# Feed-forward of an encoder layer on one core: one pass over three blocks of 768 tokens becomes two passes through DRAM, with the down-projection as seven products

## The chip, the cores and the metric

The kernel runs on one core of a Trainium2 chip. The metric is the time of the device in microseconds; three runs of the kernel before gave 3423.46, 3423.21 and 3426.85, median 3423.46. The engines are called PE (matmul), DVE (vector), ACT (scalar), POOL or GpSimd, and SP (here it only issues DMAs).

## The reference, cut to what matters

One encoder layer over 2304 tokens (a prompt of 2048 and a sample of 256) of width 1024. The change concerns its second half:

```python
x = x + jnp.concatenate([m_out, a_out], axis=-1) @ w_out
h = rmsnorm(x, norm2_w)
u = centred_dwconv(h @ w_up, conv_w, conv_b)      # 1024 -> 5632, width-3 convolution over tokens
a, g = jnp.split(u, 2, axis=-1)                   # value and gate, 2816 each
return x + (jax.nn.silu(g) * a) @ w_down          # then the final rmsnorm
```

## The kernel before, in words

Everything is transposed: channels on the 128 partitions, tokens along the free axis. Each fp32 operand of a matmul is split into a high half (an ACT copy to the matmul's type) and a low half (a DVE subtraction), and each product is three matmuls: high by high, high by low, low by high.

Phases A and B make the attention and mLSTM heads. **Phase C** (L1041) multiplies by W_out in nine blocks of 256 tokens, adds the residual, stores x and the second norm (x1_d, n2_d), and `n2_sums` makes the sums of the norm that the next phase needs (n2t_d).

**Phase D** is the feed-forward: three blocks of 768 tokens, in each 11 groups. A group is two gate channels blocks and two value channel blocks of 128, so two calls of `up`. A call of `up` multiplies two channel blocks by Strassen's scheme (Winograd's form): instead of eight half-sized products it makes seven, named 11, 21, t2, t1, t3, 22, t4 in that order, each of 12 matmuls. Their operands are quarters of the weight pair or sums of quarters (GpSimd makes four sums, L1189 to L1192, tiles tw; the raw pair lies in tiles ru) and of the normed activations (seven operands kept for the whole block; three are loaded EARLY, during phase C, four LATE, L1127). Products 11 and 21 need only the first tile of the pair; t2 and all later ones need GpSimd's sums or the second tile. PSUM sums are combined into u by ACT copies (L1200) and DVE adds (L1203). The convolution is one ACT operation (L1271) and two DVE operations (L1278), then Silu on the gate (L1352) and the multiplication (L1358). The result is split (L1363, L1364) and multiplied by w_down directly: 96 matmuls a group (L1322), whose sums DVE adds to the block's accumulators (L1324). This down-projection is held back by one group (`pend`), so that it lies between the up-projections of the next. `finish` makes the final norm of a block.

What sets the order: each engine executes its own queue strictly in order, and a scheduler places the instructions in these queues when the program is built. Tiles of one tag rotate through a ring of `bufs` buffers: a new tile waits until the last use of the tile that had its buffer. The rings here: raw 4 (RW; w_up pairs and w_down tiles), tw 3, split weights wu 5 (WU), y 3 (YB).

## Time and profile before

| | |
|---|---|
| median of three runs | 3423.46 us |
| span of the profiled execution | 3427.2 us |
| PE busy | 3329.3 us, 97% |
| DVE busy | 2677.3 us, 78% |
| ACT busy | 1931.2 us, 56% |
| POOL busy | 1120.9 us, 33% |
| last run of W_out matmuls begins, first up-projection matmul behind it | 1825.77 us, 1830.45 us |
| DMA, mean over the span | 118 GB/s |

For the profiled execution the profile gives the span and no other time. Times in a row of the timeline are start and duration in us. A group's row gives the line in the program, engine, operation, the tiles written and read, shapes and count, then busy time, the mean in ns, and the idle time ahead of them with what ended it. SPq and POOLq are the DMA issues of SP and GpSimd. Busy times of PE overlap at their ends, since matmuls are pipelined.

### The profile page before, as it was taken

The page shows a single profiled execution, that of the slowest core. Times are in us where ns is not written, and L with a number is a line of the kernel's source. Part 1 is how long each engine was busy: PE and PEld are TensorE (multiplying, and loading weights), DVE is VectorE, ACT ScalarE, POOL GpSimd, SP SyncE. Part 2 cuts the span into 40 slices and gives each one's busy share as a digit, 9 for nine tenths or more (in the row PEclk, how much of TensorE's full clock was granted, in tenths as well). Part 3 has the DMA queues.
Part 4 walks back from the last instruction along what each step waited for, and adds up shares of the span by engine and source line. Part 5 has one row for each costly group of instructions (what it writes and reads, how often), then busy time and mean ns, then how long its engine had stood idle before and what let it go on. Part 6 is the DMA issues. An engine that isn't in the chain of part 4 may idle for free. (4 is left out here: it accounts for less than half of the span.)

```text
span 3427.2 us, 55596 instructions
## 1 busy us (share of the span) xinstructions
PE 3329.3 (97%) x20058; PEld 3098.4 (90%) x20058; DVE 2677.3 (78%) x4654; ACT 1931.2 (56%) x4329; POOL 1120.9 (33%) x1328
## 2 busy tenths in 40 slices
PE   7989999999999999899999999999999999999998
PEld 6878888888888888688899999999999999999998
DVE  6885687777768788967767878789888888888776
ACT  4536666666666767655544444446444446555554
POOL 6653132213232323211244333226233224322222
PEclk9999999999999999999999999999999999999999
DMA  6765342333345444422365232223323213421221
GB/s 220 243 203 159 89 140 86 115 123 98 108 131 160 143 123 139 145 77 94 101 216 198 81 105 87 68 80 133 129 94 103 72 59 128 140 74 62 69 74 50
DMA packets 254756, 404.27 MB, mean 118 GB/s; under 512 B 32112, under 2 KB 156816, under 8 KB 254480
## 3 DMA queue, kind: packets, MB, share of 16 engines
q1 hardware_dynamic: 226576, 358.23, 32.7%
q0 software_dynamic: 11344, 33.04, 3.6%
q10 hardware_dynamic: 16560, 9.44, 0.9%
q8 instruction: 158, 2.59, 0.3%
q14 instruction: 118, 0.97, 0.1%
HBM read 316.73 MB, written 83.90 MB: 117 GB/s over the span
## 5 line engine op out<-in xcount | busy, mean ns | idle before, releaser
L1322 PE MATMUL pd<-act,wd 128*128 128x384 f32 (+1 forms) x3120 | 593.4, 336 | 23.9 <-DVE acc L1324 12.6
L1322 PEld LDWEIGHTS pd<-act,wd 128*128 128x128 f32 x3120 | 539.6, 188 | 32.6 <-DVE acc L1324 18.1
L601 DVE TENSOR_TENSOR pl<-ps,ph 128x512 fp32r<-128x512 f32 x520 | 352.7, 683 | 181.5 <-ACT ps L600 173.4
L1184 PE MATMUL pa<-nt,wut 128*128 128x386 f32 (+2 forms) x2376 | 454.3, 339 | 0.0
L599 ACT ACTIVATE ph<-ps 128x512 fp32r<-128x512 f32 x520 | 309.4, 595 | 243.5 <-PE ps L596 239.5
L1184 PEld LDWEIGHTS pa<-nt,wut 128*128 128x128 f32 x2376 | 421.6, 190 | 0.3 <-ACT u L1200 0.3
L570 DVE TENSOR_REDUCE mx<-px 128x1 f32<-128x512 f32 (+1 forms) x528 | 345.5, 670 | 74.4 <-PE px L569 72.4
L1278 DVE SCALAR_TENSOR_TENSOR y<-u,cw,y 128x768 f32<-128x768 f32 (+1 forms) x264 | 315.6, 1196 | 36.4 <-ACT y L1271 29.3
L1189 POOL TENSOR_TENSOR tw<-ru 128x512 f32<-128x512 f32 x66 | 94.1, 1425 | 732.5 <-DMA ru<-w_up 558.5
L613 PE MATMUL pv<-ph,v 128*128 128x512 f32 (+1 forms) x1040 | 319.4, 401 | 1.0 <-ACT ph L599 0.8
L600 ACT ACTIVATE ps<-ps 128x512 f32<-128x512 f32 x520 | 310.3, 597 | 0.0
L1200 ACT ACTIVATE u<-pa 128x386 f32<-128x386 f32 (+2 forms) x264 | 128.3, 486 | 320.9 <-PE pa L1184 320.7
L1324 DVE TENSOR_TENSOR acc<-pd,acc 128x384 f32<-128x384 f32 (+1 forms) x544 | 280.3, 535 | 35.5 <-PE pd L1322 34.1
L1041 PEld LDWEIGHTS po<-cmx,wo 128*128 128x128 f32 x1728 | 220.7, 191 | 8.2 <-DVE mmx L931 0.6
L1041 PE MATMUL po<-cmx,wo 128*128 128x256 f32 x1728 | 224.2, 284 | 0.4 <-DVE mmx L931 0.4
L595 PE MATMUL ps<-qq,kk 128*128 128x512 f32 x520 | 215.5, 416 | 4.2 <-DVE mx L570 2.4
L569 PE MATMUL px<-kk,qq 128*128 128x512 f32 (+1 forms) x528 | 202.8, 413 | 6.0 <-DVE mx L570 2.9
L596 PE MATMUL ps<-qm,kl 65*128 65x512 f32 x520 | 206.7, 399 | 0.0
L759 PE MATMUL mj<-mn,wm 128*128 128x256 f32 x1296 | 203.0, 289 | 2.8 <-ACT og L773 1.9
L759 PEld LDWEIGHTS mj<-mn,wm 128*128 128x128 f32 x1296 | 187.1, 193 | 19.8 <-ACT og L773 2.0
L769 PEld LDWEIGHTS mv<-wm,mn 128*128 128x128 f32 x1296 | 182.8, 190 | 18.4 <-ACT qb L765 2.5
L769 PE MATMUL mv<-wm,mn 128*128 128x256 f32 x1296 | 196.5, 285 | 1.0 <-ACT qb L765 0.9
(288 smaller groups left out, 7266.6 us busy)
## 6 DMA issues: line engine op xcount, KB each, us to landing
ru<-w_up SPq DMA_DIRECT2D x132, 512.0 KB, 3.4
mn<-n_d SPq DMA_DIRECT2D x216, 256.0 KB, 3.4
rd<-w_down SPq DMA_DIRECT2D x66, 512.0 KB, 3.6
n_d<-n1T SPq DMA_DIRECT2D x18, 1024.0 KB, 5.6
dm<-nm_d POOLq DMA_DIRECT2D x72, 256.0 KB, 4.1
mjn<-n_d SPq DMA_DIRECT2D x72, 256.0 KB, 3.3
mvn<-n_d SPq DMA_DIRECT2D x72, 256.0 KB, 3.1
q_d<-qz SPq DMA_DIRECT2D x18, 512.0 KB, 3.7
```

The lines of the kernel that those rows point to most:

```text
L570: nc.vector.tensor_reduce(s.mx[:, t, z0:z0 + 1], ps[:, 0:w], AX.X, ALU.max)
L599: nc.scalar.activation(ph, ps, AF.Exp)
L600: nc.scalar.activation(ps, ps, AF.Exp)
L601: nc.vector.tensor_tensor(pl, ps, f32(ph), ALU.subtract)
L613: nc.tensor.matmul(s.pv[0:HD if k in (1, 3) else P, 0:N], v, p, start=(kp == 0 and k == 0), stop=(2 * kp + 2 == s.nk and k == 5))
L759: nc.tensor.matmul(pj[:, o], s.w[c][:, a, o * P:(o + 1) * P], nT[c][:, :, h, :], start=(c + o + k == 0), stop=(c == NCC - 1 and k == 2 and ...
L769: nc.tensor.matmul(pv[:, o], nT[c][:, o, a, :], s.w[c][:, h, 256:512], start=(c + o + k == 0), stop=(c == NCC - 1 and k == 2 and o == 1))
L1041: nc.tensor.matmul(po[:, o], wo[z // 2][c][:, a, n], mx[c][:, h, :], start=(c == 0 and k == 0), stop=(c == NCC - 1 and k == 2))
L1184: nc.tensor.matmul(p, w[:, aa, c, :], ops[k][:, c, bb, 0:n], start=c == 0 and i == 0 and not add, stop=c == NCC // 2 - 1 and i == 2, skip_ ...
L1278: nc.vector.scalar_tensor_tensor(y[:, s:e], u[:, s + k:e + k], cw[:, k, jj:jj + 1], y[:, s:e], ALU.mult, ALU.add)
L1322: nc.tensor.matmul(po, wds[j][c // 4][:, aa, c % 4 * P:(c % 4 + 1) * P], acts[j][:, bb, z0:z1], start=(j == 0 and k == 0), stop=(j == len( ...
L1324: nc.vector.tensor_tensor(accs[c][:, z0:z1], po, accs[c][:, z0:z1], ALU.add)
```

## The change

The feed-forward becomes two passes. `phase_u` runs over two blocks of 1152 tokens and makes only the up-projections, the convolutions and the products of gate and value. For every group GpSimd makes four sums of quarters of these products (L1325 to L1330, tiles tc) and issues seven stores to DRAM (a_d, L1311). In block 2 (b = 1) it also loads the group's two w_down tiles (rd, L1240), makes four sums of them (td, L1242 to L1245) and stores seven quarters and sums (s_d, L1247). `phase_e` then makes the down-projection as seven products over all tokens, three column thirds each, with weights and activations read back from s_d and a_d, halves made by ACT and DVE, and four quadrant accumulators in SBUF; residual and final norm follow in the same loop.

A product of the up-projection is now two column halves of 290 (block 1) or 286 columns (block 2), 24 matmuls. The first tile of a w_up pair has its own ring of two; the second tile shares a ring of two with the w_down tiles of block 2. The tiles tw and td share a ring of three, wu has four buffers. u22 is added straight from PSUM. x1_d has another layout. The stores of `n2_sums` are issued by GpSimd in halves of the columns.

```diff
-BLK = 768
+BLK = 1152
-WU = 5
+WU = 4
-NH = 386
+NH = 580
-DT = (0, 2 * NH, 2 * NH + BLK, T)
+DT = (0, 2 * NH, T)
+HB = BLK // 2
+TW = T // 2
+NP = NFC // 2
+CG = 384
-WD = 4
+WR = 13
+TR = 4
+TG = 4
+WA = 2
...
-def up_load(g, s1, b, jj):
-    rs = [s1.tile([P, D], F32, tag="raw", name=f"ru{b}_{jj + k}", bufs=RW) for k in range(2)]
-    for k, r in enumerate(rs):
-        g.nc.sync.dma_start(r, g.w_up[jj + k].rearrange("p c n -> p (c n)"))
-    return rs
+def up_load(g, pool, b, jj, k):
+    r = pool.tile([P, D], F32, tag="raw", name=f"ru{b}_{jj + k}", bufs=2)
+    g.nc.sync.dma_start(r, g.w_up[jj + k].rearrange("p c n -> p (c n)"))
+    return r
...
@@ up_start
-    r1, r2 = rs or up_load(g, s1, b, jj)
+    r1 = rs or up_load(g, s1, b, jj, 0)
...
-        for c in range(NCC // 2):
-            for i, (aa, bb) in enumerate(((0, 0), (0, 1), (1, 0))):
-                nc.tensor.matmul(p, w[:, aa, c, :], ops[k][:, c, bb, 0:n], start=c == 0 and i == 0 and not add,
-                                 stop=c == NCC // 2 - 1 and i == 2, skip_group_check=add)
+        for z in range(2):
+            for c in range(NCC // 2):
+                for i, (aa, bb) in enumerate(((0, 0), (0, 1), (1, 0))):
+                    nc.tensor.matmul(p[:, z], w[:, aa, c, :], ops[k][:, c, bb, z * m:z * m + m],
+                                     start=c == 0 and i == 0 and not add, stop=c == NCC // 2 - 1 and i == 2,
+                                     skip_group_check=add)
...
-    def rest(u1, u2):
+    def rest(u1, u2, sr):
+        r2 = up_load(g, sr, b, jj, 1)
+        a21, a22 = r2[:, 0:h], r2[:, h:D]
+        t1, t2, t4 = (sr.tile([P, h], F32, tag="tmp", name=f"tw{k}_{nm}", bufs=3) for k in (1, 2, 4))
+        nc.gpsimd.tensor_tensor(t1, a21, a22, ALU.add)
+        nc.gpsimd.tensor_tensor(t2, t1, a11, ALU.subtract)
+        nc.gpsimd.tensor_tensor(a21, a11, a21, ALU.subtract)
+        nc.gpsimd.tensor_tensor(t4, a12, t2, ALU.subtract)
...
-        copy(u22, p1)
-        add(u22, u22, u21)
+        add(u22, p1, u21)
...
+DOPS = ("11", "t2", "21", "t3", "t1", "22", "t4")
+def down_sums(g, s1, gi):
+    nc = g.nc
+    h = D // 2
+    r1, r2 = (s1.tile([P, D], F32, tag="raw", name=f"rd{gi}_{k}", bufs=2) for k in range(2))
+    for k, r in enumerate((r1, r2)):
+        nc.sync.dma_start(r, g.w_down[0, (2 * gi + k) * P:(2 * gi + k + 1) * P, :])
+    t1, t2, t4 = (s1.tile([P, h], F32, tag="tmp", name=f"td{k}_{gi}", bufs=3) for k in (1, 2, 4))
+    nc.gpsimd.tensor_tensor(t1, r1[:, h:D], r2[:, h:D], ALU.add)
+    nc.gpsimd.tensor_tensor(t2, t1, r1[:, 0:h], ALU.subtract)
+    nc.gpsimd.tensor_tensor(r1[:, h:D], r1[:, 0:h], r1[:, h:D], ALU.subtract)
+    nc.gpsimd.tensor_tensor(t4, r2[:, 0:h], t2, ALU.subtract)
+    for k, t in enumerate((r1[:, 0:h], t2, r2[:, 0:h], r1[:, h:D], t1, t4, r2[:, h:D])):
+        nc.gpsimd.dma_start(g.s_d[k, gi], t)
...
@@ the loop over groups (phase_d becomes phase_u)
+            def store(k, gi, t):
+                nc.gpsimd.dma_start(g.a_d[gi // TG][DOPS.index(k), :, gi % TG, b * HB:(b + 1) * HB], t)
             for gi, gr in enumerate(groups):
...
+                for y, yg in zip(yas, ygs):
+                    nc.vector.tensor_tensor(y, y, yg, ALU.mult)
+                b11, b12, b21, b22 = (y[:, k * HB:(k + 1) * HB] for y in yas for k in range(2))
+                t1, t2, t4 = (sp.tile([P, NH], F32, tag="tc", name=f"tc{k}_{b}_{gi}", bufs=3)[:, 0:HB] for k in (1, 2, 4))
+                store("11", gi, b11)
+                nc.gpsimd.tensor_tensor(t1, b12, b11, ALU.subtract)
+                nc.gpsimd.tensor_tensor(t2, b22, t1, ALU.subtract)
+                for k, t in (("t2", t2), ("21", b21), ("t1", t1)):
+                    store(k, gi, t)
+                nc.gpsimd.tensor_tensor(b12, b22, b12, ALU.subtract)
+                nc.gpsimd.tensor_tensor(t4, b21, t2, ALU.subtract)
+                for k, t in (("t3", b12), ("22", b22), ("t4", t4)):
+                    store(k, gi, t)
+                if b:
+                    down_sums(g, sr, gi)
...
+def phase_e(g, tc, pd):
...
+        def halves(t):
+            lo, hi = t[:, 1], t[:, 0]
+            nc.scalar.activation(hi, f32(lo), AF.Copy)
+            nc.vector.tensor_tensor(lo, f32(lo), f32(hi), ALU.subtract)
+        def weight(i, p):
+            w = sw.tile([P, 2, h], F32R, tag="w", name=f"we{k}_{p}", bufs=WR)
+            nc.sync.dma_start(f32(w[:, 1]), g.s_d[i, p])
+            halves(w)
...
+        def acts(i, z, q):
+            t = sx.tile([P, 2, TG, CG], F32R, tag="t", name=f"te{DOPS[i]}_{z}_{q}", bufs=TR)[:, :, 0:p1 - p0]
+            nc.sync.dma_start(f32(t[:, 1]), g.a_d[q][i, :, :, z * CG:(z + 1) * CG])
+            halves(t)
...
+        for i, k in enumerate(DOPS):
+            for z in range(G3):
...
+                for p in range(NP):
+                    if p % TG == 0:
+                        fetch_t(1)
+                    mul(p, range(4))
+                    if i == 0 and z == 0 or z == G3 - 1:
+                        fetch_w(1)
...
+                for m in range(2):
+                    update(m)
```

What the scheduler makes of it, at three places. First SP, at the end of phase C. Before: cx_22522 is the last block of W_out; nt and n are the late operands of block 1, ru_25 a w_up tile of the second pair.

```order
L1127 DMA nt_0_23046<-n2t_d 128x2x386 x2
L1050 DMA x_d<-cx_22522 128x1024
L1127 DMA nt_0_23047<-n2t_d 128x2x386 x2
L1127 DMA n_0_23048<-n_d 128x2x386 x2
L1127 DMA nt_0_23049<-n2t_d 128x2x386 x2
L1158 DMA ru_25_23350<-w_up 128x1024
L1065 DMA n_d<-cx_22522 128x4x256 x2
```

Now: cx_22564 is the last block, ru_23 the second tile of the first pair.

```order
L1066 DMA n_d<-cx_22246 128x4x256 x2
L1051 DMA x_d<-cx_22564 128x4x256 x2
L1066 DMA n_d<-cx_22564 128x4x256 x2
L1128 DMA nt_0_23100<-n2t_d 128x2x580 x2
L1128 DMA nt_0_23101<-n2t_d 128x2x580 x2
L1128 DMA n_0_23102<-n_d 128x2x580 x2
L1128 DMA nt_0_23103<-n2t_d 128x2x580 x2
L1161 DMA ru_23_23136<-w_up 128x1024
L1161 DMA ru_1_23360<-w_up 128x1024
```

The last block's stores to n2_d stood behind the late operands, and stand ahead of them now; the first pair's second tile has moved from phase C to behind the late operands.

Second, DVE between two groups. Here in block 1 of the change: wu and wut of 40 are low halves of the next gate pair (27318 product 11, 27345 product 21, 27385 product t2, 27414 product t1), y_16 the first value convolution of the group that ends, L1321 its multiplication with the gate.

```order
L1187 TENSOR_TENSOR wu_0_40_27318<-ru_40_27314,wu_0_40_27318 128x512
L1214 TENSOR_TENSOR u_17_27135<-pa_16_27078,u_17_27135 128x580
L1187 TENSOR_TENSOR wu_0_40_27345<-ru_40_27314,wu_0_40_27345 128x512
L1214 TENSOR_TENSOR u_16_27134<-pc_16_27175,u_16_27134 128x580
L1187 TENSOR_TENSOR wut_0_40_27385<-tw_0_40_27377,wut_0_40_27385 128x512
L1302 SCALAR_TENSOR_TENSOR y_16_27289<-u_16_27134,cw,y_16_27289 128x1151
L1302 SCALAR_TENSOR_TENSOR y_16_27289<-u_16_27134,cw,y_16_27289 128x1152
L1187 TENSOR_TENSOR wut_0_40_27414<-tw_0_40_27376,wut_0_40_27414 128x512
L1321 TENSOR_TENSOR y_16_27289<-y_16_27289,y_38_27065 128x1152
```

And the same place in block 2, with y_16 and y_17 the two value convolutions, pb_40 the PSUM sum of product 21 of the next gate pair, 32822 its product t2, 32851 its t1:

```order
L1302 SCALAR_TENSOR_TENSOR y_16_32700<-u_16_32545,cw,y_16_32700 128x1152
L1302 SCALAR_TENSOR_TENSOR y_16_32700<-u_16_32545,cw,y_16_32700 128x1151
L1321 TENSOR_TENSOR y_16_32700<-y_16_32700,y_38_32468 128x1152
L1214 TENSOR_TENSOR u_40_32809<-pb_40_32754,u_40_32809 128x572
L1302 SCALAR_TENSOR_TENSOR y_17_32709<-u_17_32546,cw,y_17_32709 128x1152
L1302 SCALAR_TENSOR_TENSOR y_17_32709<-u_17_32546,cw,y_17_32709 128x1151
L1321 TENSOR_TENSOR y_17_32709<-y_17_32709,y_39_32477 128x1152
L1187 TENSOR_TENSOR wut_1_40_32822<-tw_1_40_32814,wut_1_40_32822 128x512
L1187 TENSOR_TENSOR wut_1_40_32851<-tw_1_40_32813,wut_1_40_32851 128x512
```

In the kernel before, the low half of t2 stands between the first convolution's two operations:

```order
L1278 SCALAR_TENSOR_TENSOR y_16_26684<-u_16_26597,cw,y_16_26684 128x767
L1181 TENSOR_TENSOR wut_0_40_26892<-tw_0_40_26850,wut_0_40_26892 128x512
L1278 SCALAR_TENSOR_TENSOR y_16_26684<-u_16_26597,cw,y_16_26684 128x768
L1203 TENSOR_TENSOR u_17_26598<-u_17_26598 128x386
L1324 TENSOR_TENSOR acc_2_23040<-pd_7_2_0_26749,acc_2_23040 128x384
L1181 TENSOR_TENSOR wut_0_40_26909<-tw_0_40_26849,wut_0_40_26909 128x512
```

In block 2 it stands behind both convolutions and both multiplications, and behind the addition that reads product 21's sum.

Third, GpSimd in block 2. Tiles 32 and 33 are the next group's gate pair, y_8 and y_9 the products of the group that ends, rd and td with _4 its w_down tiles and their sums.

```order
L1242 TENSOR_TENSOR td_4_30753<-rd_0_30749,rd_1_30750 128x512
L1247 DMA s_d<-rd_1_30750 128x512 x2
L1243 TENSOR_TENSOR td_4_30754<-td_4_30753,rd_0_30749 128x512
L1244 TENSOR_TENSOR rd_0_30749<-rd_0_30749 128x512
L1247 DMA s_d<-td_4_30753 128x512
L1245 TENSOR_TENSOR td_4_30755<-rd_1_30750,td_4_30754 128x512
L1247 DMA s_d<-td_4_30754 128x512
L1247 DMA s_d<-rd_0_30749 128x512
L1247 DMA s_d<-td_4_30755 128x512
L1203 TENSOR_TENSOR tw_1_32_30829<-ru_33_30827 128x512
L1311 DMA a_d_66<-y_8_30716 128x576
L1325 TENSOR_TENSOR tc_1_4_30735<-y_8_30716 128x576
```

SP has, in that stretch, the second w_down tile ahead of the gate pair's second tile:

```order
L1161 DMA ru_32_30767<-w_up 128x1024
L1240 DMA rd_0_30749<-w_down 128x1024
L1161 DMA ru_10_30999<-w_up 128x1024
L1240 DMA rd_1_30750<-w_down 128x1024
L1161 DMA ru_33_30827<-w_up 128x1024
L1161 DMA ru_11_31059<-w_up 128x1024
```

In the kernel before, GpSimd has in a group only the weight sums of the two pairs:

```order
L1189 TENSOR_TENSOR tw_0_16_26558<-ru_17_26555 128x512
L1190 TENSOR_TENSOR tw_0_16_26559<-tw_0_16_26558,ru_16_26554 128x512
L1191 TENSOR_TENSOR ru_17_26555<-ru_16_26554,ru_17_26555 128x512
L1192 TENSOR_TENSOR tw_0_16_26560<-ru_16_26554,tw_0_16_26559 128x512
L1189 TENSOR_TENSOR tw_0_40_26849<-ru_41_26846 128x512
L1190 TENSOR_TENSOR tw_0_40_26850<-tw_0_40_26849,ru_40_26845 128x512
L1191 TENSOR_TENSOR ru_41_26846<-ru_40_26845,ru_41_26846 128x512
L1192 TENSOR_TENSOR tw_0_40_26851<-ru_40_26845,tw_0_40_26850 128x512
```

GpSimd's queue now has w_down sums, their stores and the activation's store between two pairs' sums.

312 lines of the change are left out of this document (172 added, 140 removed).

## The prediction

> **What bounds the kernel now.** I read the busy shares, the span's costliest groups, then the feed-forward's windows, since the change lies almost wholly there.
>
> ```profile
> span 3427.2 us, 55596 instructions
> PE 3329.3 (97%) x20058; PEld 3098.4 (90%) x20058; DVE 2677.3 (78%) x4654; ACT 1931.2 (56%) x4329; POOL 1120.9 (33%) x1328
> 2182.00:2228.40 46.40, 46.40 (x266) 46.40 (x265) 37.08 (x53) 21.71 (x40) 12.50 (x9) 1.00 0.21 69
> 3100.00:3146.00 46.00, 46.00 (x266) 46.00 (x265) 36.54 (x52) 24.40 (x52) 11.87 (x9) 1.00 0.21 69
> ```
>
> A window row gives start:end, its length, busy time of PE, weight loads, DVE, ACT and POOL, the granted clock, DMA share and GB/s. One group of two pairs fills such a window: PE is busy for all of it at clock 1.00, DVE for 80%. TensorE decides, so a matmul removed is time gained, as long as the others still feed it.
>
> ```profile
> 2242.22 1.57 DVE L1358 TENSOR_TENSOR y<-y,y 128x768 f32<-128x768 f32 x1
> 2288.72 1.57 DVE L1358 TENSOR_TENSOR y<-y,y 128x768 f32<-128x768 f32 x1
> 2820.02 1.58 DVE L1358 TENSOR_TENSOR y<-y,y 128x768 f32<-128x768 f32 x1
> 2979.96 1.13 DVE L1358 TENSOR_TENSOR y<-y,y 128x768 f32<-128x768 f32 x1
> 3380.28 10.83 PE L1322 MATMUL pd<-act,wd 128*128 128x256 f32 x90
> ```
>
> The product of gate and value ends each group, so the first two starts give the period: 46.5 us (46.45 over several groups). By the code a group has 168 up and 96 down matmuls of about 385 columns: 176 ns each. The last row gives 256 columns: 90 in 10.83 us, less some 0.16 by which an end lags, 118.6 ns. Time goes with columns, 0.443 ns each, and not with instructions.
>
> **The matmuls.** Up: 5544 become 7392 of 290 and 286 columns, the same columns in all. By the two points above these take 133.6 and 131.9 ns, so a group of 336 takes 44.9 us in block 1 and 44.3 in block 2, and 22 groups 981 us; strict proportion to 386 columns would give 972, to 256 columns 993. Down: 3168 matmuls of 384 (556 us at 175.5 ns) become 2772: 486.5 us. So PE's own gain is 70 us; two blocks in place of three also drop one block change: 2820.0 to 2980.0 is three groups, 139, and 21 us more. What remains is whether PE is fed.
>
> **Phase C to the first up-projection.**
>
> ```profile
> 1825.77 4.84 PE L1041 MATMUL po<-cmx,wo 128*128 128x256 f32 x39
> 1830.45 2.29 PE L1184 MATMUL pa<-n,wu 128*128 128x386 f32 x12
> 1839.59 1.14 PE L1184 MATMUL pc<-nt,wut 128*128 128x386 f32 x5 [0.92 <-POOL nt L1129]
> 1830.64 0.89 SPq L1127 DMA_DIRECT2D nt<-n2t_d  x2
> 1834.97 1.12 SPq L1127 DMA_DIRECT2D nt<-n2t_d  x2
> 1843.79 1.92 SPq L1065 DMA_DIRECT2D n_d<-cx  x2
> 1832.14 1.28 POOL L1054 TENSOR_TENSOR cacc<-cacc,csq 128x512 f32<-128x512 f32 x1 [4.46 <-ACT csq L1052]
> 1840.23 1.07 POOL L135 TENSOR_TENSOR rcol_c<-rcol_c,mhalf 128x2 f32<-128x2 f32 x1 [0.70 <-DMA nt<-n2t_d]
> 1841.36 0.71 PE L142 MATMUL rs_c<-ident,rcol_c 128*128 128x128 f32 x4 [0.28 <-POOL rcol_c L135]
> 1842.11 3.22 DVE L1063 SCALAR_TENSOR_TENSOR cx<-cx,nw,rs_c 128x256 f32<-128x256 f32 x8 [0.48 <-PE rs_c L142]
> 1836.00:1842.00 6.00, 4.81 (x29) 4.17 (x28) 4.63 (x6) 4.78 (x9) 3.49 (x4) 1.00 1.04 368
> ```
>
> Now the late operands' loads are issued as the last W_out matmul ends (1830.5), ahead of the last norm's stores (1843.8), and PE has three early products to run meanwhile; the gaps sum to some 3 us. In the changed order SP issues the last stores first, then the eight late loads (594 KB each), then the pair's second half, and the early products 11 and 21 (6.4 us) have moved ahead of the last W_out matmuls. So PE's next product, t2, waits for the whole chain: residual, square and GpSimd sums to 3.8 us after the end of W_out, two visits to PE (0.5, 0.7) with the root between (1.07) and small steps, 2.9, eight scalings 3.2: 9.9; then 1.05 MB of stores and 5.3 MB of loads at the 368 GB/s of the window above, 17.2, then two GpSimd sums and two halves, 4.2: 31 us, and 1.6 for the clock (below). I take 33; 25 if the loads overlap the stores, 41 if GpSimd's late halves come before its sums. The early products lose nothing, they are only done sooner.
>
> **Clock.** After a gap of PE the granted clock falls:
>
> ```profile
> 2404.00:2406.00 2.00, 2.00 (x7) 2.00 (x7) 2.00 (x3) 0.51 (x1) 0.00 (x0) 0.50 0.60 242
> 2403.44 3.77 PE L1184 MATMUL pc<-n,wu 128*128 128x384 f32 x12
> 2407.74 2.27 PE L1184 MATMUL pa<-nt,wut 128*128 128x384 f32 x12
> ```
>
> The same twelve matmuls took 1.5 us longer after the gap; I add 1.6 for each gap of some us.
>
> **Block 1.** DVE, ACT and GpSimd serve a group of 44.9 us.
>
> ```profile
> L1278 DVE SCALAR_TENSOR_TENSOR y<-u,cw,y x264: 997/1018/2303, 1853.0 to 3386.4; 128x768 f32<-128x768 f32 x88, 128x767 f32<-128x767 f32 x44
> L1203 DVE TENSOR_TENSOR u<-pc,u 128x386 f32<-128x386 f32 x2 | 1.1, 562 | 2.1 <-PE pc L1184 2.1
> L1358 DVE TENSOR_TENSOR y<-y,y x6: 941/1258/1581, 2187.0 to 2288.7; 128x768 f32<-128x768 f32 x6
> L1181 DVE TENSOR_TENSOR wut<-ru,wut 128x512 fp32r<-128x512 f32 x4 | 2.7, 683 | 1.3 <-ACT wut L1180 1.3
> L1181 DVE TENSOR_TENSOR wut<-tw,wut 128x512 fp32r<-128x512 f32 x4 | 3.8, 958 | 0.2 <-ACT wut L1180 0.2
> L1180 ACT ACTIVATE wut<-tw 128x512 fp32r<-128x512 f32 x4 | 2.5, 624 | 0.9 <-PE pc L1184 0.9
> ```
>
> A convolution step of 1152 is 1.5 us (1.018 x 1.5), a sum of 580 from PSUM 0.8, a low half 0.68, a product of gate and value 1.41 (0.941 x 1.5). DVE per group: 14 low halves 9.5, six PSUM sums 4.8, eight steps 12, two products 2.8: 29 us. GpSimd: eight weight sums, four activation sums and seven stores, at the prices of the rows further down 13, 7 and 4: 24 us. It fits, with waits: a ring of three y tiles now frees only when GpSimd's stores have landed. I allow 7 us for 11 groups (0 to 35). The block change reloads seven operands with no down-projection to run meanwhile: 8 us (0 to 25).
>
> **Block 2** is the largest term. Two things stand between product 21 and product t2 of every gate pair. Call E the end of the group before on PE; products 11 and 21 keep PE busy until E + 6.4.
>
> First, DVE's order. In block 2 it has, after the sum from product 21 (E + 6.4), the second convolution and the multiplication, and only then t2's low half: 0.8 + 2 x 1.5 + 1.4 + 0.7 gives E + 12.3. In block 1 that low half comes before both. So PE waits at least 5.9 us, whatever GpSimd does.
>
> Second, the rings.
>
> ```profile
> ru<-w_up SPq DMA_DIRECT2D x132, 512.0 KB, 3.4
> rd<-w_down SPq DMA_DIRECT2D x66, 512.0 KB, 3.6
> L1189 POOL TENSOR_TENSOR tw<-ru 128x512 f32<-128x512 f32 x64 | 91.5, 1430 | 729.2 <-DMA ru<-w_up 555.1 <-DVE acc L1324 114.7 <-DVE wu L1181 22.1
> L1190 POOL TENSOR_TENSOR tw<-tw,ru 128x512 f32<-128x512 f32 x64 | 108.3, 1693 | 5.2 <-POOL tw L1189 0.7
> L1191 POOL TENSOR_TENSOR ru<-ru,ru 128x512 f32<-128x512 f32 x64 | 112.5, 1757 | 0.0
> L637 POOL DMA_DIRECT2D mix_d<-o x56: 532/577/708, 280.7 to 1775.3; - x56
> DMA to landing us min/median/max: 2.0/2.9/7.6
> ```
>
> The second half of a w_up pair and both w_down tiles share two buffers. The second w_down load waits for the last low half of the value pair, which waits for a buffer of the ring of four, free when the fourth product from the end starts (E - 12.7), and takes 0.62 and 0.68: E - 11.4, or E - 10.5 with a DVE operation ahead of it. Load 3.6, four sums of 1.4 to 1.75 with four stores of 0.58 between: the store of the tile's changed half is issued at E + 0.8 to 2.2, lands 2.9 later; then the next pair's load 3.4, its first sum 1.43, a store and an activation sum (576 columns, 1.5 to 1.75, from the 512-column rows) queued ahead, the second sum 1.69 and a high half 0.62: E + 12.3 at the least times, E + 14.7 at the means. So PE waits 5.9 to 8.4 and loses 1.6 to the clock, 7.5 to 10 for each of 10 changes of group. I take 8.5: **85 us** (60 to 115, with a queue behind GpSimd or a better overlap than I see).
>
> **The second pass and the tail.** Its first operand's halves stand behind the last convolutions: 14 us (6 to 22). Then 486.5 us, and 5 for its column changes. Its loads (65 MB by the tile sizes) come to some 135 GB/s, well below the 368 of the window above.
>
> ```profile
> 3411.24 0.71 PE L142 MATMUL rs_d<-ident,rcol_d 128*128 128x128 f32 x4
> 3406.14 17.99 SPq L1313 DMA_DIRECT2D yT<-acc  x24
> ```
>
> The last norm leaves 16 us after the last product, as now. Phases A to C stay; that norm-2 sums are stored by GpSimd in smaller pieces I cost at nothing, since W_out's matmuls cover it (1 to 3 us if not).
>
> **Sum**: 1830.5 + 33 + 981 + 7 + 8 + 85 + 14 + 486.5 + 5 + 16 = 3466 against the profiled 3427.2. The three runs' median, 3423.46, lies 3.7 lower, so 3462.
>
> **Rivals.** (a) *PE alone decides in block 2*: operands are ready, the 85 us are not lost: 3377. For it: PE is now 97% busy, GpSimd 33%. Against it: the order of DVE, which is fixed. The change gains when the loss per group is below 4.7 us (3462 - 3423.5 = 38.5; 85 - 38.5 = 46.5 over ten). Chance 0.15, with smaller losses at the boundaries. (b) *DVE and GpSimd exclude each other.* The convolution step's maximum, 2303, is its minimum plus a whole GpSimd sum of 1.3, and low halves of tw tiles take 958 against 683. If each excludes the other, a group needs 24 us of such DVE work and 16 of GpSimd sums with 512 columns at the 1.28 of the fence above, in block 1 (40 of 44.9; now, by the same count, 35 of 46.4), and with the w_down sums 45 of 44.3 in block 2. If nearly each op then waits, block 1 takes 48 (+34 us) and block 2 a little more: 3500. Chance 0.15. The Trainium skill (SBUF — State Buffer, Who interferes with whom) states this lock for a DVE operation with two SBUF inputs against a GpSimd one that reads SBUF; the two means agree. (c) *GpSimd's stores are held up by DVE.* Held for one DVE step each, 2.3 us at the most, 14 stores per group of block 2 would put 32 us more on GpSimd, in all 67 for a group of 53: 150 us more, 3610. The issue rows show 532 to 708 ns in 56 stores with DVE at work, so 0.03. The Trainium skill (SBUF — State Buffer, SBUF: two separate sides) has such a store go from 620 to 3100 ns beside a copy on DVE; no row here shows that. (d) *Gains and losses cancel*: 5.5 us per group and 25 at the boundary: 3462 - 30 - 8 = 3424. Chance 0.06. That the change does not do what it says is excluded for the matmuls, whose count and columns the order shows.
>
> **How the numbers follow.** The forecast has 0.61, its own range 3430 to 3495. Two kernels of this length are told apart at about 0.2% (7 us). Faster: (a), 0.15, and a little of (d), 0.01. Within 0.2%: most of (d) and the forecast's low edge, 0.08. Slower: the rest, 0.76. The range holds the forecast, (b) and (d), 3412 to 3512; (a) with its whole gain and (c), 0.18, lie outside.
>
> **What would show it.** In the changed profile: PE idle some 30 us after the last W_out matmul, released by GpSimd's weight sum or DVE's low half; block 1's period near 45 with clock 1.00; block 2's period near 53, with one gap of 6 to 8 us per group before t2 of the gate pair and the clock at half behind it; second pass near 490 with PE full; tail 16. Wrong if block 2's period is below 49, if block 1's is above 46.5, or if the 290-column matmuls take above 140 ns.

## The result, and the profile after

The changed kernel takes 3544.26 us (median of four runs, 3540.94 to 3550.11), the kernel before 3424.09: ratio 1.0348, interval 1.0333 to 1.0362. It is slower, as forecast, but by 120 us in place of 38, and outside the range (3412 to 3512). The profiled execution spans 3545.5 us, against 3427.2; the forecast on that scale was 3466, so 79.5 us have to be found.

The page of the changed kernel, its busy shares and the groups of the up-projection and the convolution:

```profile
span 3545.5 us, 57329 instructions
PE 3303.1 (93%) x21402; PEld 3070.1 (87%) x21402; DVE 2476.5 (70%) x3748; ACT 1775.9 (50%) x3702; POOL 1366.6 (39%) x1652
L1191 PE MATMUL pa<-nt,wut 128*128 128x290 f32 (+1 forms) x3168 | 476.1, 308 | 134.2 <-ACT wut L1186 130.1
L1302 DVE SCALAR_TENSOR_TENSOR y<-u,cw,y 128x1152 f32<-128x1152 f32 (+1 forms) x176 | 362.5, 2060 | 52.4 <-ACT yc L1300 36.7
```

PE went from 97% to 93%, with 134 us of idle time at one place, the products that read a weight sum (wut), waiting for ACT's high half of it. A convolution step takes 2060 ns in the mean; its shortest is 1.40.

Windows of the changed kernel: one group of block 1, one of block 2, the block change, the second pass (columns as in the prediction).

```profile
2240.00:2285.00 45.00, 45.00 (x337) 45.00 (x336) 36.79 (x30) 21.14 (x32) 25.39 (x19) 1.00 0.28 94
2583.00:2641.00 58.00, 47.66 (x336) 47.07 (x336) 38.87 (x30) 23.61 (x45) 28.75 (x30) 0.88 0.37 122
2357.00:2424.00 67.00, 55.55 (x391) 53.74 (x389) 63.48 (x39) 37.08 (x52) 48.31 (x27) 0.96 0.56 187
3090.00:3500.00 410.00, 409.80 (x2379) 409.48 (x2378) 198.97 (x183) 126.85 (x130) 95.05 (x50) 1.00 0.53 168
```

Block 1 and the second pass are full. A group of block 2 has 336 matmuls in 58 us, where PE alone needs 44.5 (below), at a mean clock of 0.88.

PE's timeline at the seams, in order of time: W_out, the first t2, one gate pair of block 2, the first matmuls of the second pass, the last norm.

```profile
1824.40 19.72 PE L1042 MATMUL po<-cmx,wo 128*128 128x256 f32 x149 [16.15 <-DVE cx L1049]
1848.12 13.56 PE L1042 MATMUL po<-cmx,wo 128*128 128x256 f32 x111
1897.02 0.85 PE L1191 MATMUL pa<-nt,wut 128*128 128x290 f32 x2 [28.76 <-ACT wut L1186]
2641.62 0.85 PE L1191 MATMUL pa<-nt,wut 128*128 128x286 f32 x2 [10.36 <-ACT wut L1186]
3038.91 1.01 PE L1454 MATMUL e<-te,we 128*128 128x384 f32 x2 [8.06 <-ACT te L1353]
3536.62 1.65 PE L143 MATMUL r<-ident,rcol 128*128 128x128 f32 x6 [1.26 <-POOL rcol L1417]
```

W_out ends at 1861.7 (1848.12 + 13.56). The terms of the prediction against these rows and, for the groups, against the starts of product 21 of each gate pair on PE:

| term | predicted, us | measured, us |
|---|---|---|
| end of W_out, with products 11 and 21 of the first pair ahead of it | 1836.9 | 1861.7 |
| from there to the first t2 | 33 | 35.3 |
| a group of block 1 | 44.9, and 7 in all for waits | 45.24 |
| block change, above the groups' own time | 8 | 17 |
| a group of block 2, PE alone | 44.3 | 44.5 |
| same, loss at a change of group | 8.5 | 13.4 |
| same, ten changes | 85 | 134 |
| to the second pass | 14 | 8 |
| second pass | 491.5 | 492 |
| tail | 16 | 14 |

The differences add up to 77 of the 79.5 us. Three carry it: 49 in block 2, 25 in phase C, 9 at the block change.

**What ends the wait in block 2.** The same stretch on DVE, ACT, GpSimd and SP, 2624 to 2643 (the second row takes the first apart: minimum, median and maximum in ns):

```profile
2632.03 8.25 DVE L1302 SCALAR_TENSOR_TENSOR y<-u,cw,y 128x1152 f32<-128x1152 f32 x2
L1302 DVE SCALAR_TENSOR_TENSOR y<-u,cw,y x2: 1419/4108/6796, 2632.0 to 2638.9; 128x1152 f32<-128x1152 f32 x1, 128x1151 f32<-128x1151 f32 x1
2640.38 0.66 ACT L1306 ACTIVATE y<-u,yc,cw 128x1 f32<-128x1 f32 x2 [8.45 <-DVE y L1302]
2640.95 1.13 ACT L1186 ACTIVATE wut<-tw 128x512 fp32r<-128x512 f32 x2
2624.17 1.31 POOL L1245 TENSOR_TENSOR td<-rd,td 128x512 f32<-128x512 f32 x1
2625.50 12.46 SPq L1161 DMA_DIRECT2D ru<-w_up  x3
2629.91 1.54 POOL L1203 TENSOR_TENSOR tw<-ru 128x512 f32<-128x512 f32 x1 [2.89 <-DMA ru<-w_up]
2633.33 1.27 POOL L1204 TENSOR_TENSOR tw<-tw,ru 128x512 f32<-128x512 f32 x1
2636.33 1.27 POOL L1206 TENSOR_TENSOR tw<-ru,tw 128x512 f32<-128x512 f32 x1
```

GpSimd has t2's sum at 2634.6, but PE gets the high half only at 2641.6. ACT has that half behind a two-column correction of the second convolution (L1306), which waits for DVE's two convolution steps; these take 8.25 us in place of 2 x 1.4. Of that the first takes 6.80 and the second 1.42: from the start of the first to 2637.6 GpSimd makes four sums with hardly a break, and the step ends 1.2 us behind the last of them. It is so at all ten changes of group (6.3 to 6.9 us). So the queue's order holds the half back, and the meeting of DVE and GpSimd makes that longer.

The rows also show what the load of the gate pair's second tile waits for: SP issues it at 2625.50, as GpSimd's fourth w_down sum ends (2624.17 + 1.31), and so within 0.04 us at all ten changes. It does not wait for a store to land.

**What ends the wait in phase C.** SP and DVE of the changed kernel:

```profile
1802.49 3.98 SPq L1149 DMA_DIRECT2D rn<-n_d  x2
1808.62 3.35 SPq L1066 DMA_DIRECT2D n_d<-cx  x4
1814.76 6.63 SPq L1033 DMA_DIRECT2D cx<-xT  x4
1823.57 1.29 DVE L1049 TENSOR_TENSOR cx<-po,cx 128x512 f32<-128x512 f32 x2 [13.23 <-DMA cx<-xT]
```

The sums of the norm are made in sixteen loads (rn) in place of eight, through the same two buffers. The last of them stand on SP ahead of the norm's stores of two blocks, and these ahead of the residual's loads (cx<-xT) for the last two blocks. PE has its PSUM buffers back only when DVE has added that residual.

**What ends the wait behind W_out.** GpSimd, at the first t2:

```profile
1890.00 3.75 POOL L1130 TENSOR_TENSOR nt<-nt 128x1160 fp32r<-128x1160 f32 x1
1893.71 1.26 POOL L1203 TENSOR_TENSOR tw<-ru 128x512 f32<-128x512 f32 x1
```

The second w_up tile has landed at 1889.0, but GpSimd has its four late low halves ahead, the last of them here, and begins the weight sums 4.7 us later.

### The profile page after: what moved, and what is told of

It reads as the page before. It is cut to its first block, busy times and chain, and to the rows that moved or that the text cites. A ratio compares the mean times of both kernels' runs of the same rounds, so it can differ in the third digit from the quotient of the medians.

```text
span 3545.5 us, 57329 instructions
## 1 busy us (share of the span) xinstructions
PE 3303.1 (93%) x21402; PEld 3070.1 (87%) x21402; DVE 2476.5 (70%) x3748; ACT 1775.9 (50%) x3702; POOL 1366.6 (39%) x1652
## 5 line engine op out<-in xcount | busy, mean ns | idle before, releaser
L1191 PE MATMUL pa<-nt,wut 128*128 128x290 f32 (+1 forms) x3168 | 476.1, 308 | 134.2 <-ACT wut L1186 130.1
L1191 PEld LDWEIGHTS pa<-nt,wut 128*128 128x128 f32 x3168 | 456.5, 200 | 141.1 <-ACT wut L1186 132.7
L1302 DVE SCALAR_TENSOR_TENSOR y<-u,cw,y 128x1152 f32<-128x1152 f32 (+1 forms) x176 | 362.5, 2060 | 52.4 <-ACT yc L1300 36.7
L1454 PE MATMUL et<-tet,wet 128*128 128x384 f32 x1584 | 276.6, 334 | 0.0
L1454 PEld LDWEIGHTS et<-tet,wet 128*128 128x128 f32 x1584 | 274.4, 188 | 0.0
L1042 PE MATMUL po<-cmx,wo 128*128 128x256 f32 x1728 | 224.7, 284 | 16.5 <-DVE cx L1049 16.1
L1454 PE MATMUL e<-te,we 128*128 128x384 f32 x1188 | 211.1, 338 | 8.8 <-ACT te L1353 8.1
L1454 PEld LDWEIGHTS e<-te,we 128*128 128x128 f32 x1188 | 208.8, 190 | 9.6 <-ACT te L1353 8.3
L614 PE MATMUL pv<-pl,v 128*128 128x512 f32 x520 | 190.7, 399 | 0.0
```

Of the source, the lines that this page charges most:

```text
L614: nc.tensor.matmul(s.pv[0:HD if k in (1, 3) else P, 0:N], v, p, start=(kp == 0 and k == 0), stop=(2 * kp + 2 == s.nk and k == 5))
L1042: nc.tensor.matmul(po[:, o], wo[z // 2][c][:, a, n], mx[c][:, h, :], start=(c == 0 and k == 0), stop=(c == NCC - 1 and k == 2))
L1191: nc.tensor.matmul(p[:, z], w[:, aa, c, :], ops[k][:, c, bb, z * m:z * m + m], start=c == 0 and i == 0 and not add, stop=c == NCC // 2 - 1 ...
L1302: nc.vector.scalar_tensor_tensor(y[:, s:e], u[:, s + k:e + k], cw[:, k, jj:jj + 1], y[:, s:e], ALU.mult, ALU.add)
L1454: nc.tensor.matmul(ps[m // 2][:, m % 2], w[:, aa, m * P:(m + 1) * P], t[:, bb], start=p == 0 and n == 0, stop=p == NP - 1 and n == 2)
```

## The experiments

A single run gives one time; spans of the profiles are compared below, with 3545.5 for the changed kernel. The kernel before took 3427.2 to 3431.8 beside these runs.

**Where block 2's time goes.** First the ring.

```diff
-    r1, r2 = (s1.tile([P, D], F32, tag="raw", name=f"rd{gi}_{k}", bufs=2) for k in range(2))
+    r1, r2 = (s1.tile([P, D], F32, tag="raw", name=f"rd{gi}_{k}", bufs=3) for k in range(2))
-    r = pool.tile([P, D], F32, tag="raw", name=f"ru{b}_{jj + k}", bufs=2)
+    r = pool.tile([P, D], F32, tag="raw", name=f"ru{b}_{jj + k}", bufs=2 + k)
```

> The changed kernel with one buffer more (three) for the ring that the second w_up tile shares with the two w_down tiles. Theory 1 (the ring of two makes the next gate pair's sums late, and so its halves stand behind the convolutions on ACT and DVE): block 2's period falls from 58.0 to 45 to 47 us, the 10 us gap before each gate pair's t2 goes, total 3545 - 120 = about 3425. Rival (DVE and GpSimd exclude each other, and block 2 simply has too much work for the two): the same work is there, so the period stays at 52 or more, total 3485 or more.

Measured: span 3447.1, 98 us less. The multiplications that end two groups of block 2, and a group's window:

```profile
2652.31 1.36 DVE L1321 TENSOR_TENSOR y<-y,y 128x1152 f32<-128x1152 f32 x1 [0.19 <-ACT y L1306]
2697.80 1.36 DVE L1321 TENSOR_TENSOR y<-y,y 128x1152 f32<-128x1152 f32 x1 [0.19 <-ACT y L1306]
```

```profile
2606.80:2652.30 45.50, 44.67 (x336) 44.21 (x335) 38.04 (x30) 23.28 (x45) 35.93 (x30) 1.00 0.46 156
```

The period is 45.5, the clock 1.00. DVE and GpSimd have the same operations as before, so their amount is not what bounds block 2. In the order of DVE, t2's low half now stands ahead of both convolutions. About 22 of the 120 us were given back at once, at the start of the second pass: that gap rose from 8 to 30 us (below).

> The changed kernel with the w_down tiles loaded, summed and stored in block 1 in place of block 2, the ring of two kept. Theory 1 (the shared ring, wherever it is): block 1's period rises from 45.2 to 55 to 60 us and block 2's falls from 58.0 to 45 to 46, total within 15 us of 3545. Rival (something that only block 2 does, its carried columns and the corrected columns at the sequence's end): block 2 stays above 50, and the total is above 3590.

```diff
-                if b:
+                if not b:
                     down_sums(g, sr, gi)
```

Measured: block 1's period rises to 55.4 in the mean, block 2's falls to 44.5; span 3524.4, 21 us less, so a little more than the 15 that theory 1 allowed. The loss goes with the w_down sums and is not of block 2's own making. It is smaller there (gaps of 4.6 to 6.2 and of 2.1 us in each group), and the block change is worse, with a gap of 22 us.

Then the issuer of the stores, with the ring of two as it was:

```diff
-                nc.gpsimd.dma_start(g.a_d[gi // TG][DOPS.index(k), :, gi % TG, b * HB:(b + 1) * HB], t)
+                g.st.dma_start(g.a_d[gi // TG][DOPS.index(k), :, gi % TG, b * HB:(b + 1) * HB], t)
-        nc.gpsimd.dma_start(g.s_d[k, gi], t)
+        g.st.dma_start(g.s_d[k, gi], t)
```

> The changed kernel with the first pass's stores (activation sums and w_down sums) issued by SP in place of GpSimd, and all else the same. Theory (an issue costs GpSimd 0.56 us, GpSimd is not what block 1 waits for): block 1's period stays at 45.2; in block 2 GpSimd is relieved of 14 issues of 0.56 us but the ring is the same, so 54 to 60. Rival (GpSimd's issuing makes the loss): block 2's period falls below 50.

Measured: span 3458.5, 87 us less. The rival holds in the mean: block 2's period is 48.7 to 50.5, in the mean 49.3. PE's row at t2, and GpSimd's w_down sums:

```profile
2654.74 0.52 PE L1191 MATMUL pa<-nt,wut 128*128 128x286 f32 x2 [1.18 <-ACT wut L1186]
2689.59 1.29 POOL L1242 TENSOR_TENSOR td<-rd,rd 128x512 f32<-128x512 f32 x1 [15.29 <-DMA rd<-w_down]
2693.79 1.29 POOL L1245 TENSOR_TENSOR td<-rd,td 128x512 f32<-128x512 f32 x1
2695.53 0.96 SPq L1161 DMA_DIRECT2D ru<-w_up  x2
```

In the changed kernel the four sums and the three issues between them took 6.7 us (2676.43 to 2683.16), with the next pair's load right behind; here the sums take 5.5. There an issue and an activation sum also stood between the pair's first two weight sums, and here nothing does: t2's sum is ready 6.5 us after the group's end in place of 9.4. With this, the planner put t2's low half ahead of the second convolution:

```
L1321 TENSOR_TENSOR y_16_32700<-y_16_32700,y_38_32468 128x1152
L1187 TENSOR_TENSOR wut_1_40_32822<-tw_1_40_32814,wut_1_40_32822 128x512
L1187 TENSOR_TENSOR wut_1_40_32851<-tw_1_40_32813,wut_1_40_32851 128x512
L1214 TENSOR_TENSOR u_40_32809<-pb_40_32754,u_40_32809 128x572
L1187 TENSOR_TENSOR wut_1_40_32879<-ru_41_32811,wut_1_40_32879 128x512
L1302 SCALAR_TENSOR_TENSOR y_17_32709<-u_17_32546,cw,y_17_32709 128x1152
```

The gap before t2 fell from 10.4 to 1.2 us. So a few microseconds on a chain through GpSimd, earned either by a buffer or by another issuer, are worth 9 to 12 us a group, and in both runs t2's halves have another place in two queues. How much of the 10.4 us the order alone makes, and how much the slow convolution steps in it, no run separated: from the rows above, 5.4 us are the excess of 8.25 over 2 x 1.4, and 5 the rest.

**Phase C.**

```diff
-                n2_sums(g, sp, 0, sums.pop(0), tag="rn", bufs=2)
+                n2_sums(g, sp, 0, sums.pop(0), tag="rn", bufs=3)
```

> The changed kernel with three in place of two buffers for the halves of the norm that GpSimd sums in phase C. Theory (the sixteen loads of these halves, each waiting for a buffer, hold up SP, and behind them stand the norm's stores and the residual's loads of the last two W_out blocks): the gap of 16 us in W_out at 1808 to 1824 shrinks to 5 or less, total 15 to 25 us less, 3520 to 3530. Rival (the GpSimd-issued stores themselves land late): the gap stays within 3 us of 16.

Measured: span 3524.9, 20.6 less. The gap of 16 us has become two of 4.2 and 3.4, and the residual's load is issued at 1795 in place of 1815:

```profile
1799.78 1.01 PE L132 MATMUL rs_c<-ones,cacc 128*128 128x2 f32 x4 [4.17 <-POOL cacc L1058]
1804.23 5.66 PE L1042 MATMUL po<-cmx,wo 128*128 128x256 f32 x30 [3.44 <-DVE cx L1049]
1795.22 1.85 SPq L1033 DMA_DIRECT2D cx<-xT  x2
```

GpSimd still issues the stores, so the queue behind the two buffers was the cause of most of it. The first t2 comes at 1879.8, 17 us earlier and still 10 later than predicted, 7.6 of them in the two gaps. The other 3 of the 20.6 us lie in block 2, where one period came out at 54.9; nothing in the trace ties that to this change.

**The boundary to the first pass.** The order of the pools decides which memory of phase C a tile lies over, and so what its load waits for. First late operands, second w_up tiles, y, u:

```diff
-        sr = st.enter_context(tc.tile_pool(name="d_2", bufs=1, reuse_waits="tile"))
-        sa = st.enter_context(tc.tile_pool(name="d_a", bufs=1, reuse_waits="tile"))
         sl = st.enter_context(tc.tile_pool(name="d_l", bufs=1, reuse_waits="tile"))
+        sr = st.enter_context(tc.tile_pool(name="d_2", bufs=1, reuse_waits="tile"))
+        sa = st.enter_context(tc.tile_pool(name="d_a", bufs=1, reuse_waits="tile"))
```

> The changed kernel with its four SBUF pools of the first pass taken in another order (late operands first), so that the second tile of the first w_up pair no longer waits for phase C's last tiles and is loaded ahead of the last norm's stores; the late operands are still behind them. Theory (stores, then loads, then sums, one after the other, make the 35 us at the boundary): t2 starts some 10 us after the last W_out matmul, the rest waits for the late operands, total idle of PE there about 20, total 3545 - 15 = 3530. Rival (the late operands alone set the end of this wait): within 4 us of 3545.

Measured: span 3547.4, so the total agrees with the rival, but not its reason. The first pass starts 8 us earlier (group 1's second multiplication at 1941.3 against 1949.6), with t2 early and a wait of 12 us for the late operands; the gap before the second pass rose by 9 us, from 8 to 17, and took it back. There the first activation tile's load stands behind thirteen weight loads on SP, lands at 3033.8, and ACT makes its high half only at 3039.1, behind the corrections of the last convolution (3036.9). That this order comes from the memory under the tiles is argued, not shown. What was a gain of 8 us is only seen by its place.

That second gap by itself, with the ring of three: the second pass's activation tiles get their pool first, over operands that are done early.

```diff
+        sx = st.enter_context(tc.tile_pool(name="e_t", bufs=1, reuse_waits="tile"))
         sw = st.enter_context(tc.tile_pool(name="e_w", bufs=1, reuse_waits="tile"))
...
-        sx = st.enter_context(tc.tile_pool(name="e_t", bufs=1, reuse_waits="tile"))
```

> The ring of three, and in the second pass the pool of the activation tiles placed first, over operands of block 2 that are done with 13 us before its end (in the run ring3 they lay over the last convolved tile). Theory (a load of the second pass waits for the last user of the memory under it: GpSimd's stores of the last group in ring3): the gap before the second pass falls from 30 us to 3 to 10, total 3447 - 22 = about 3425. Rival (the last group's w_down sums and their stores are what is waited for): the gap stays above 20.

In the run ring3, and then here:

```profile
2941.36 1.01 PE L1454 MATMUL e<-te,we 128*128 128x384 f32 x2 [30.33 <-ACT te L1353]
2934.06 2.69 SPq L1368 DMA_DIRECT2D te<-a_d  x4
2933.92 0.56 POOL L1311 DMA_DIRECT2D a_d<-y  x1
```

```profile
2924.39 6.65 PE L1454 MATMUL e<-te,we 128*128 128x384 f32 x22 [14.21 <-ACT we L1353]
2899.81 32.13 SPq L1359 DMA_DIRECT2D we<-s_d  x11
2923.15 0.66 ACT L1306 ACTIVATE y<-u,yc,cw 128x1 f32<-128x1 f32 x2 [3.39 <-DVE y L1302]
2923.72 0.61 ACT L1353 ACTIVATE we<-we 128x512 fp32r<-128x512 f32 x1
```

In ring3 the load of te is issued as GpSimd comes to its last stores of the group's product: one buffer more in an early pool had shifted the pools behind it, and te lay over that tile. Here the gap is 14.2 us, span 3430.6, 16.5 less: the cause was right, and the 3 to 10 us were missed. What ends the 14.2 is no load: the first weight is loaded from 2899.8 and has landed at 2909.4, but ACT has its high half behind the correction of the last convolution (L1306), which waits for DVE's steps until 2923.15.

All three together, with the pools in the order y, late operands, second w_up tiles, u:

```diff
-        sr = st.enter_context(tc.tile_pool(name="d_2", bufs=1, reuse_waits="tile"))
         sa = st.enter_context(tc.tile_pool(name="d_a", bufs=1, reuse_waits="tile"))
         sl = st.enter_context(tc.tile_pool(name="d_l", bufs=1, reuse_waits="tile"))
+        sr = st.enter_context(tc.tile_pool(name="d_2", bufs=1, reuse_waits="tile"))
         sp = st.enter_context(tc.tile_pool(name="d_s", bufs=2, reuse_waits="tile"))
```

> Ring of three, three buffers for phase C's norm sums, and the first pass's pools in the order y tiles, late operands, second w_up tiles, u tiles: the first pair's second tile is loaded ahead of the last norm's stores, and the second pass's first activation tiles lie over late operands. If the gains of the single runs add up (98, 20, about 10 at the boundary, 20 at the second pass): 3545 - 148 = 3397. If one is only handed on to the next wait: above 3415.

Measured: span 3398.8, 147 us less than the changed kernel, so the gains add up; the gap before the second pass is 7.1 us.

With that, the late operands' pool last, and the activation tiles of the second pass first as above:

```diff
-        sr = st.enter_context(tc.tile_pool(name="d_2", bufs=1, reuse_waits="tile"))
         sa = st.enter_context(tc.tile_pool(name="d_a", bufs=1, reuse_waits="tile"))
-        sl = st.enter_context(tc.tile_pool(name="d_l", bufs=1, reuse_waits="tile"))
         sp = st.enter_context(tc.tile_pool(name="d_s", bufs=2, reuse_waits="tile"))
+        sr = st.enter_context(tc.tile_pool(name="d_2", bufs=1, reuse_waits="tile"))
+        sl = st.enter_context(tc.tile_pool(name="d_l", bufs=1, reuse_waits="tile"))
```

> As the run before, with the late operands' pool last in place of second, and the activation tiles of the second pass first: SP now issues the late operands ahead of the last norm's stores and the first pair's second tile behind both. Theory of the boundary (stores, loads and sums in one chain of 33 us; the loads' 14 us move under the norm's chain): idle of PE there falls from 35 to 20 to 24, total 3385 to 3400. Rival (the second w_up tile, which is still last, sets it, behind the same stores): 30 or more stays.

Measured: span 3406.2; the boundary as predicted:

```profile
1848.93 1.22 PE L143 MATMUL rs_c<-ident,rcol_c 128*128 128x128 f32 x4 [3.60 <-POOL rcol_c L136]
1867.26 0.85 PE L1191 MATMUL pa<-nt,wut 128*128 128x290 f32 x2 [17.10 <-ACT wut L1186]
```

PE is idle for 21 us there, against 33.5 in the changed kernel and 30 in norm_ring3. The late loads are issued at 1841.0 to 1847, beside the norm's chain, and no longer behind its stores. Against norm_ring3 the second group's gate pair comes to its product 21 at 1911.7 in place of 1923.5, 12 us sooner, of which 3.6 are there already when W_out ends. So the new order is worth 8 of the 14 us of the loads; no run accounts for the other 6, though GpSimd's late halves still stand ahead of its sums (2 us of it, below). The total misses its 3400 because the gap before the second pass is 14.2 us again.

**The sum of the repairs.** The next two have all of that, with the second pass's pools in the order weights, accumulators, x, and the activation tiles last, and differ in the issuer of the stores.

```diff
-        sx = st.enter_context(tc.tile_pool(name="e_t", bufs=1, reuse_waits="tile"))
...
         sy = st.enter_context(tc.tile_pool(name="e_x", bufs=1, reuse_waits="tile"))
+        sx = st.enter_context(tc.tile_pool(name="e_t", bufs=1, reuse_waits="tile"))
```

> Ring of three, three buffers for phase C's norm sums, late operands' pool last in the first pass (loaded ahead of the last norm's stores), and the second pass's activation tiles placed over the late operands that are done first; GpSimd issues the stores. Theory (each wait was one of buffers, and no other takes its place): boundary as in late_operands_first (21 us idle), block 2 at 45.5, gap before the second pass 7 to 9: 3385 to 3395, 1% faster than the kernel before. Rival (the gap before the second pass is set by the last convolutions on ACT and DVE, wherever the tiles lie): 14 us stay there, 3400 to 3405.

Measured: 3401.03 us (median of four) against 3428.23, ratio 0.992 (0.9902 to 0.9938). Its profiled execution spans 3395.9, above the 3385 to 3395 of the theory. The gap before the second pass is 7.1, so the rival's 14 do not stay; but the rival has the mechanism, since here too the wait ends on ACT: the activation tile has landed at 2881.9, and its high half is made at 2889.0, behind the first operation of the last convolution. With the tiles in this order ACT comes to it sooner.

> The same with the first pass's stores issued by SP. Theory (with a ring of three the sums are early enough, so the issuer no longer matters): within 8 us of the run with GpSimd's stores. Rival (GpSimd's 14 issues of 0.56 us still delay its sums, and block 2's 45.5 falls to 44.5): 10 us or more less.

Measured: 3388.36 us, ratio 0.9884 (0.9866 to 0.9902), span 3383.7, 12 less. The rival holds: block 2's period is 44.5, PE's own time, against 45.5 to 46.8. Nine periods are 13 us shorter together, and the block change is 1 us longer. Block 1 stays at 45.3 in the mean with either.

**The block change.** The same kernel with GpSimd's share of the reloaded operands' halves given to DVE:

```diff
-P1 = ((V, G),) * 7
+P1 = ((V, V),) * 7
```

> The run all_sp_stores with the low halves of block 2's seven reloaded operands all made by DVE (half of them are GpSimd's there). Theory (at the block change DVE's operations of 0.68 us take up to 3.1 because GpSimd's halves of 2.5 us lock it out; the 21 us are this): DVE gets 7 x 1.33 = 9 us more work and loses the waits, the block change falls from 21 to 8 to 14 us, total 3384 - 10 = 3374. Rival (DVE has too much to do there, whoever holds the lock): the block change stays at 19 or grows.

In the changed kernel, DVE's low halves at the block change took up to 3.1 us, beside GpSimd's halves:

```profile
2383.89 3.14 DVE L1187 TENSOR_TENSOR wut<-ru,wut 128x512 fp32r<-128x512 f32 x1
2386.95 3.11 DVE L1187 TENSOR_TENSOR wu<-ru,wu 128x512 fp32r<-128x512 f32 x1
```

```profile
L1130 POOL TENSOR_TENSOR nt<-nt x4: 2883/3167/3776, 2386.6 to 2418.5; 128x1144 fp32r<-128x1144 f32 x4
```

With all halves on DVE, the same kind of operation (minimum, median, maximum) and the window of the block change:

```profile
L1187 DVE TENSOR_TENSOR wu<-ru,wu x6: 676/686/1919, 2333.0 to 2390.3; 128x512 fp32r<-128x512 f32 x6
```

```profile
2330.00:2395.00 65.00, 60.12 (x444) 59.22 (x443) 61.75 (x54) 40.71 (x58) 27.65 (x14) 1.00 0.64 214
```

The two groups around the change take 102.0 us (61.4 + 40.6) in place of 110.7 (65.7 + 45.0), measured between the multiplications that end a group. By that count the loss falls from 21 to 12; between the gate pairs on PE, as in the table above, it falls from 19 to 10. The span is 3375.8, 8 less, so the theory holds; what makes the 10 that remain no run shows. DVE is as busy as before in that window (61.75 of 65, 61.43 in the run before) with more of its own work in it.

```diff
-P0 = ((V, G),) * 4
+P0 = ((V, V),) * 4
```

> The same, and the low halves of block 1's late operands also by DVE. At the boundary after phase C GpSimd made them in 3.4 to 3.75 us each ahead of its weight sums. Theory (they delay the sums): the idle time of PE there falls by a further 4 to 8 us. Rival (the late halves are then late on DVE): no change against the run with the reloaded operands alone.

Measured: 3375.77 us (3374.41 to 3378.46) against 3427.8, ratio 0.985 (0.9833 to 0.9866). Against the run before the span is 3372.9, 3 us less, no more than these four runs lie apart, so only its place tells: the idle time of PE at the boundary is 18.6 in place of 20.7. So the late halves on GpSimd cost some 2 us in this version, less than the 4 to 8 of the theory; the weight sums now wait for the second w_up tile's load. This version beats the kernel before by 1.5% (PE is 97% busy in it, as in the kernel before).

## Why the prediction was right or wrong

**PE's own time**: right. Proportion to columns held: a group of block 1 took 45.2 us (44.9 by the two points) and of block 2 44.5 (44.3), the second pass 492 (491.5).

**The boundary after phase C**: right in size (35.3 for 33), and in mechanism for all but its end. The second w_up tile landed 27.3 us after W_out, where 9.9 + 17.2 make 27.1. The last link, "two GpSimd sums and two halves, 4.2", took 8.1, since GpSimd's late halves came before its sums: the condition of the 41, which I had left out of the 33. The 1.6 for the clock, which falls behind t2 and not ahead of it, hid part of that. Moving the loads beside the norm's chain took 8 us out, of the 14 that 5.3 MB at 368 GB/s make; where the other 6 went stays open.

**Phases A to C at nothing**: wrong, and by 25 us. The step failed was "that norm-2 sums are stored by GpSimd in smaller pieces I cost at nothing, since W_out's matmuls cover it". W_out's matmuls cover GpSimd's sums but not what stands behind their loads on SP: the residual that these matmuls' PSUM buffers wait for. I had named no queue for this step, although it doubled the loads through a ring of two; a third buffer took 17 us of it back, and two gaps of 7.6 us together are left in W_out.

**Block 2**, the largest miss: the two causes were named rightly, their size was wrong, and so was that they stand apart. The order of the queue held t2's halves behind the convolution, and the ring made the sums late: sums made early, by a buffer or by another issuer, give 45.5 or 49 in place of 58. So "PE waits at least 5.9 us, whatever GpSimd does" failed: with earlier sums the planner itself placed the halves ahead of both convolutions or of the second, and PE did not wait at t2 (ring3) or waited 1.2 us (stores_by_sp). What was mis-sized in the sum is the row "0.8 + 2 x 1.5 + 1.4 + 0.7": the two convolution steps took 8.25 us and not 3, since the first fell together with four GpSimd sums, and the wait ended on ACT's high half behind the corrections. I had the price of such a meeting in the row of the step's maximum (2303 ns), and used it only for a rival that counted the whole group. The term for the clock was too small as well: at gaps of 10 us it was 3.2 (PE busy 47.7 in the 58 us window against 44.5) and not 1.6. GpSimd's own part I put too late: its t2 sum was ready some 9 us after the group's end, not 11.7 to 14, since the pair's load waited for the fourth w_down sum and not for a store to land.

**The block change**: 17 in place of 8, inside its 0 to 25. The step said only that seven operands are reloaded "with no down-projection to run meanwhile". What it left out is GpSimd's halves of 1144 columns, 2.9 to 3.8 us each, beside which DVE's halves of 0.68 us take up to 3.1; in the repaired kernel the loss was 19 with them and 10 without.

**Rival (b)**, DVE and GpSimd excluding each other, was right as a local price at these two places and wrong as a bound on a group: with the same operations block 2 ran at 45.5. **Rival (c)** had stores held up by DVE; an issue took 0.54 to 0.60 us, as priced, so that is out. Its kin was missed: the issues stand between the sums on one queue, and on the chain to t2's sum four of them stood, with an activation sum; in the version without them the planner found another order. **Rival (a)** did not happen in the change, but is what the repaired version does: 44.5 us a group.

**The direction**, slower, came out as forecast. **The range** left out 3544 because two terms passed their own bounds: block 2 with 134 for 60 to 115, and phase C with 25 for nothing, or 1 to 3. Both bounds were drawn from the same view as their values.

## What to carry to other kernels

When a ring is shared by two streams, follow the chain from the last reader of one to the first use of the other, with every instruction that the queues put between, DMA issues too; a few microseconds there can move an operation behind a whole stage in a queue whose order is fixed when the program is built. When a step is cut into more pieces through the same buffers, look at what stands behind its loads on their queue, however idle the engine that works on them. And when memory is laid out anew, ask of each first load of the next phase which tile it lies over and who reads that last, and of each first operand what stands ahead of its halves on ACT and DVE: an added buffer in one pool moved a wait of 22 us to another phase, and with that mended ACT's order still held 14.

## What the runs showed of the hardware

A DVE operation that reads two tiles in SBUF took its own time plus that of GpSimd's operations beside it: 3.1 us for a low half of 0.68 beside halves of 2.9 to 3.8, and 6.8 for a convolution step of 1.4 beside four sums of 1.3 to 1.4 (5.2 together). The Trainium skill (SBUF — State Buffer, Who interferes with whom) has the port pair that the two share as an exclusive lock, and a DVE instruction with two SBUF inputs contending with a GpSimd one that reads SBUF; taking GpSimd's halves away from the block change brought the median low half from 1.25 us back to 0.69, which agrees. It did not make GpSimd and DVE time add up over a group: in the best version DVE is busy for 34.8 us and GpSimd for 27.2, together 62, of a period of 44.5.

A store of 256 or 288 KB issued by GpSimd cost it 0.54 to 0.60 us, 0.56 also in the midst of the step of 6.8 us on DVE, and landed in a median of 2.7 us for 288 KB.
